# A hybrid decoder layer on one core: key and query weights loaded a pair ahead, samples' steps within the attention's filling, a copy moved to DVE

## The chip, the cores and the metric

The kernel runs on one core of a Trainium2 chip. A core has five engines that work side by side, each through its own instructions in order: PE (TensorE, the matmuls), ACT (ScalarE), DVE (VectorE), POOL (GpSimd) and SP (SyncE, which here only issues transfers). ACT and POOL issue transfers too, from the same queue of instructions in which their computing stands. All transfers are carried out by 16 DMA engines. The metric is the time of one execution in microseconds (us), the median of several runs.

## The reference

One layer is computed for two groups at once: a prompt of 512 tokens and eight samples of one token each, with shared weights. From a normed input `h`, three branches run in parallel (RG-LRU, a gated delta rule, latent attention), are merged by gates, and a feed-forward part follows. The parts that the change touches are the causal convolution of four taps and the prompt's latent attention:

```python
def causal_conv(u, buf, w):
    T = u.shape[1]
    up = jnp.concatenate([buf.astype(u.dtype), u], axis=1)
    y = up[:, 0:T] * w[0]
    for j in range(1, CONV_W):
        y = y + up[:, j:j + T] * w[j]
    return y, up[:, T:]

def mla_prompt_attention(q_nope, q_rope, c_kv, k_rope, w_ukv):
    kv = jnp.einsum('bsc,cf->bsf', c_kv, w_ukv).reshape(B, S, H, QK_NOPE + V_HEAD)
    k_nope, v = kv[..., :QK_NOPE], kv[..., QK_NOPE:]
    ...
    s = (q_nope @ k_nope + q_rope @ k_rope) * MLA_SCALE      # 8 heads, causal
    p = softmax(s)
    return p @ v
```

The samples attend to 4096 cached positions each, in 128-row pages of `cache_ckv` and `cache_krope` that a page table names: scores against the pages, softmax, and a weighted sum of the pages, 32 pages a sample.

## The kernel before

All large products are made in three matmuls: each float32 weight tile is loaded into `raw` (two slots, `load`, L151), split by ACT into a high part `whi` (L158) and by DVE into the rest `wlo` (L159), two slots each; the activations are split in the same way (`hilo`, L179 and L180). PE then adds hi x hi, hi x lo and lo x hi in PSUM (`gemm`, L172).

Tokens lie along the free dimension, features on the 128 partitions. The stages in order of time: modulation and norm; the gated delta rule with its 24 convolutions (`prepare`), up to about 480 us; the RG-LRU branch with ten more convolutions (`lru_steps`) together with the samples' delta rule; the latents' products and the prompt's attention, about 737 to 925 us; three merges (`merge`), the output product, and the feed-forward part to the end.

The convolution (`conv`) puts 35 columns of state in front of the 512 columns of the prompt in a tile `cin` (two slots): POOL copies the state (L383), ACT the prompt (L384), DVE the samples' new column (L386); ACT and DVE then compute the four taps (L387 to L393).

The samples' attention is cut into 42 steps by a generator. `steps(n)` adds n to a count and runs as many steps as it then holds. The numbers of steps a call are `STEPS = (0.8, 0.7, 0.8, 0.7, 0.4, 1.2)`: index 5 for each pair of heads, 1 for each of the 16 rounds of the attention, 2 for the merges. A step of scores (L1112, tile `sp`) uses one block of pages in `cc`, which holds two blocks; the loads of the next block, eight of 144 KB, are issued as one becomes free: POOL issues numbers 1, 3 and 5 (`POOLED`, L1080), SP the other five (L1085). Every second step multiplies the weights with value pages (L1144, tile `sa`), which POOL loads into four tiles `cv` of 512 KB (L1127).

The latents' stage (from L1316 on) loads the stored latents `d_ck` and `d_cq` into `bf` (two slots, L1325, on SP) and splits them; `values` makes the values of all heads with `w_uv` (L1301, copied by ACT at L1303); then for each of four pairs of heads comes a key product and two query products (`lat_gemm`, L1312, two PSUM tiles `mm`), with `w_uk` (256 columns) and `w_uq` (768 columns) loaded by ACT's queue through `raw`. The key product is copied by ACT into `kt` (L1339), the query products are multiplied by DVE into `qt` (L1346).

The attention runs 18 rounds, i from -2 to 15: `attend` of round i, `turn` (transposes, L1377) of round i + 1 and `scores` (L1359, softmax at L1362 to L1367) of round i + 2. The rounds -2 and -1 fill this pipeline and end with `continue`, ahead of `steps(STEPS[1])`.

The order of each engine's instructions is not that of the text alone. A planner at build time goes by the program's order as priority, but takes what is ready by its own estimate of durations, and gives out the slots of the tiles; on the chip the order of each engine is then fixed. An instruction that waits holds all behind it on its engine. Pools that are opened later lie where closed ones lay, and their tiles wait for the last user of the place.

Of the kernel before, what the change touches and what calls it, by code (L numbers as in the profile page):

```python
# [9 lines left out]
F32 = mybir.dt.float32  # L10
# [13 lines left out]
NT = 2 * HB  # L24
# [78 lines left out]
def emit(es, tc, I, O):  # L103
# [43 lines left out]
    queue = [SP]  # L147
# [14 lines left out]
    def wload(src, n):  # L162
        return split(load(src, n), n)
# [153 lines left out]
    with ExitStack() as pha:  # L317
# [61 lines left out]
        def conv(p, pt, state, w, bias, nb, y):  # L379

            cin = p.tile([128, 548], F32, tag="cin", name="cin", bufs=2)
            y2 = p.tile([128, CW], F32, tag="cw", name="cz", bufs=6)
            G.tensor_copy(cin[:, 0:35], state)  # L383
            A.activation(view2(cin[:, 35:547]), pt[:, :, 0:256], AF.Copy)  # L384
# [902 lines left out]
    with ExitStack() as sub:  # L1287
# [5 lines left out]
        def values(lat):  # L1293
            uvs = [wload(I["w_uv"][c], 1024) for c in range(2)]
            for b in range(4):
                pt = mm_tile()
                for c in range(2):
                    xh, xl = lat["ck", c]
                    for i, (x, w) in enumerate(((xh, uvs[c][0]), (xh, uvs[c][1]), (xl, uvs[c][0]))):
                        for a in range(2):  # L1300
                            TE.matmul(pt[:, a, :], x[:, off(b):off(b) + 128], w[:, a * 512:(a + 1) * 512],  # L1301
                                      start=c == 0 and i == 0, stop=c == 1 and i == 2)
                A.activation(view2(vv[:, b]), pt, AF.Copy)  # L1303
                steps(STEPS[4])
# [11 lines left out]
        with ExitStack() as sub2:  # L1316
# [3 lines left out]
            krp = pl.tile([128, 512], F32, name="krp")  # L1320
            lat = {}
            for nm, src, n in (("ck", d_ck, 2), ("cq", d_cq, 3)):
                for i in range(n):
                    f = pl.tile([128, NT], F32, tag="bf", name="bf", bufs=2)
                    SP.dma_start(f, src[i])  # L1325
                    lat[nm, i] = hilo(pl, f, f"{nm}{i}", bufs=1)
# [7 lines left out]
            for p in range(4):  # L1334
                pt = lat_gemm(lat, wload(I["w_uk"][p], 256), 0, "ck", 2)
                kt = ph.tile([128, 2, 512], F32, name=f"kt{p}")
# [4 lines left out]
                kts.append(kt)  # L1341
                wq = wload(I["w_uq"][p], 768)
                for u in range(2):
# [49 lines left out]
        for i in range(-2, 16):  # L1393
# [7 lines left out]
            if i + 2 < 16:  # L1401
                Ps[i + 2] = scores(*order[i + 2])
            if i < 0:
                continue
            steps(STEPS[1])
            if 8 <= i < 13:
# [415 lines left out]
```

## Time and profile before

| | before |
|---|---|
| median of 3 runs | 1553.57 us (1547.87 to 1562.55) |
| profiled execution, its time | 1555.39 us |
| its span, first to last instruction | 1553.6 us |
| instructions | 33507 |
| moved by DMA | 255.98 MB, mean 165 GB/s |

The page gives the busy time of each engine over the span; the other views give the same execution by wait, by stretch of time, or instruction by instruction. The granted clock is that of PE, as a share of full speed. `ACTq` and `SPq` are the instruction queues of ACT and SP where transfers are issued.

### The profile page before, as it was taken

The page shows a single profiled execution, that of the slowest core. Times are in us where ns is not written, and L with a number is a line of the kernel's source. Part 1 is how long each engine was busy: PE and PEld are TensorE (multiplying, and loading weights), DVE is VectorE, ACT ScalarE, POOL GpSimd, SP SyncE. Part 2 cuts the span into 40 slices and gives each one's busy share as a digit, 9 for nine tenths or more (in the row PEclk, how much of TensorE's full clock was granted, in tenths as well). Part 3 has the DMA queues.
Part 4 walks back from the last instruction along what each step waited for, and adds up shares of the span by engine and source line. Part 5 has one row for each costly group of instructions (what it writes and reads, how often), then busy time and mean ns, then how long its engine had stood idle before and what let it go on. Part 6 is the DMA issues. An engine that isn't in the chain of part 4 may idle for free.

```text
span 1553.6 us, 33507 instructions
## 1 busy us (share of the span) xinstructions
PE 1479.3 (95%) x13348; PEld 1346.7 (87%) x13348; DVE 818.9 (53%) x1938; ACT 643.1 (41%) x1226; POOL 243.2 (16%) x391
## 2 busy tenths in 40 slices
PE   8999999999998999999878889999999999999997
PEld 5799999999987988887665559999999999999997
DVE  4577865857755676765344424464464333333333
ACT  4464644644533777564334433232243222222233
POOL 0121000100103444333323532000000000000001
PEclk7999999999998999999889999999999999999998
DMA  8234142351436966877777978676743223323222
GB/s 344 83 112 122 58 127 95 97 155 61 125 117 196 270 194 210 275 235 249 241 234 198 265 248 292 192 240 216 270 151 109 84 86 86 103 93 95 84 84 93
DMA packets 117774, 255.98 MB, mean 165 GB/s; under 512 B 22281, under 2 KB 53770, under 8 KB 117618
## 3 DMA queue, kind: packets, MB, share of 16 engines
q1 hardware_dynamic: 83904, 161.85, 33.0%
q0 software_dynamic: 13824, 47.72, 9.9%
q10 hardware_dynamic: 19890, 44.27, 8.8%
q8 instruction: 105, 1.72, 0.5%
q14 instruction: 51, 0.42, 0.1%
HBM read 228.61 MB, written 25.18 MB: 163 GB/s over the span
## 4 chain that ended last, share of the span: by engine, by line
PE 51%; DMA 4%; issue 2%; ACT 2%; DVE 1%; another core or an unknown queue 1%; SPq 0%; POOL 0%; ACTq 0%; POOLq 0%; DVEq 0%
PE mm L172 40%; PE sp L1112 2%; PE sa L1144 1%; DMA bf<-d_ro 1%; PE s L224 1%; PE ho L1387 1%; PE h L1359 1%; DMA St<-in_S 1%; PE mm L1312 1%; DMA bf<-d_cq 1%; PE h L1377 1%; DMA out_gS_s<-St 1%; PE s L888 1%; DMA raw<-in_w_rg 1%
## 5 line engine op out<-in xcount | busy, mean ns | idle before, releaser
L158 ACT ACTIVATE whi<-raw 128x1024 fp32r<-128x1024 f32 (+3 forms) x204 | 199.5, 979 | 506.9 <-PE mm L172 443.6
L159 DVE TENSOR_TENSOR wlo<-raw,whi 128x1024 fp32r<-128x1024 f32 (+3 forms) x204 | 229.1, 1124 | 232.4 <-ACT whi L158 226.4
L172 PE MATMUL mm<-hh,whi 128*128 128x260 f32 x1312 | 281.1, 292 | 4.9 <-ACT hh L295 2.7
L172 PE MATMUL mm<-hh,wlo 128*128 128x260 f32 x1312 | 273.5, 287 | 0.1
L172 PE MATMUL mm<-hl,whi 128*128 128x260 f32 x1312 | 272.9, 287 | 0.7 <-DVE hl L295 0.6
L172 PEld LDWEIGHTS mm<-hh,whi 128*128 128x128 f32 x1312 | 206.8, 191 | 16.6 <-issue 7.9
L172 PEld LDWEIGHTS mm<-hl,whi 128*128 128x128 f32 x1312 | 206.1, 191 | 3.2 <-issue 2.1
L172 PEld LDWEIGHTS mm<-hh,wlo 128*128 128x128 f32 x1312 | 206.1, 191 | 3.0 <-issue 1.4
L172 PE MATMUL mm<-h2h,whi 128*128 128x260 f32 x704 | 144.5, 284 | 0.0
L172 PE MATMUL mm<-h2h,wlo 128*128 128x260 f32 x704 | 144.1, 283 | 0.0
L172 PE MATMUL mm<-h2l,whi 128*128 128x260 f32 x704 | 143.6, 283 | 0.0
L1080 POOL DMA_INDIRECT cc<-in_ckvT,pkx x96 | 101.6, 1058 | 129.6 <-PE sp L1112 74.3
L172 PE MATMUL mm<-brh,whi 128*128 128x260 f32 x556 | 114.2, 287 | 5.1 <-ACT brh L179 4.9
L172 PE MATMUL mm<-brl,whi 128*128 128x260 f32 x556 | 113.0, 284 | 0.7 <-issue 0.6
L172 PE MATMUL mm<-brh,wlo 128*128 128x260 f32 x556 | 112.3, 284 | 0.0
L172 PEld LDWEIGHTS mm<-h2h,whi 128*128 128x128 f32 x704 | 109.3, 188 | 2.9 <-issue 2.5
L172 PEld LDWEIGHTS mm<-h2h,wlo 128*128 128x128 f32 x704 | 109.4, 188 | 0.4 <-issue 0.4
L172 PEld LDWEIGHTS mm<-h2l,whi 128*128 128x128 f32 x704 | 109.1, 188 | 0.4 <-DVE h2l L1549 0.4
L172 PEld LDWEIGHTS mm<-brh,whi 128*128 128x128 f32 x556 | 86.0, 189 | 11.0 <-ACT brh L179 6.0
L172 PEld LDWEIGHTS mm<-brl,whi 128*128 128x128 f32 x556 | 85.9, 189 | 1.6 <-DVE mx L1120 0.8
L172 PEld LDWEIGHTS mm<-brh,wlo 128*128 128x128 f32 x556 | 86.0, 189 | 0.3 <-issue 0.2
L1610 POOL TENSOR_TENSOR x<-x,rf 128x260 f32<-128x260 f32 x6 | 4.3, 736 | 514.7 <-ACT rf L1607 514.7
(522 smaller groups left out, 2500.7 us busy)
## 6 DMA issues: line engine op xcount, KB each, us to landing
raw<-in_w_in SPq DMA_DIRECT2D x55, 512.0 KB
wa<-in_w_ada SPq DMA_DIRECT2D x48, 512.0 KB
cc<-in_ckvT SPq DMA_DIRECT2D x160, 144.0 KB
raw<-in_w_f SPq DMA_DIRECT2D x44, 512.0 KB
raw<-in_w_in ACTq DMA_DIRECT2D x27, 512.0 KB
raw<-in_w_f SPq DMA_DIRECT2D x16, 384.0 KB
d_g<-gt ACTq DMA_DIRECT2D x22, 260.0 KB
raw<-in_w_rg ACTq DMA_DIRECT2D x16, 320.0 KB
```

The source lines that it names most:

```text
L158: A.activation(hi[:, :n], raw[:, :n], AF.Copy)
L159: V.tensor_tensor(lo[:, :n], raw[:, :n], hi[:, :n], ALU.subtract)
L172: TE.matmul(pt[:, a, 0:HB], w[:, k * 128:k * 128 + 128], x[k0 + k][:, a * HB:(a + 1) * HB], start=start and k == 0 and i == 0, stop=stop a ...
L224: TE.matmul(pt[32 * j:32 * j + 32, 0:256], sc[:, k, :], wa[:, j * 256:(j + 1) * 256], start=k == 0, stop=k == 7)
L888: TE.matmul(pw[:, 0:272], a_[:, sl], b_[:, ca], start=i == 0, stop=i == 2)
L1080: G.indirect_dma_start(ct[:, i].rearrange("p c t -> p (c t)"), None, I["ckvT"], bass.IndirectOffsetOnAxis(ap=pkx[0:96, o:o + 1], axis=0))
L1112: TE.matmul(po[32 * j:32 * j + 32, 0:256], Qst[:, t, 4 * self.g + j, :], cts[j][:, :, t, :], start=t == 0, stop=t == 2)
L1144: TE.matmul(self.pa[32 * j:32 * j + 32, 0:256], self.PTt[:, t * 128 + 32 * j:t * 128 + 32 * j + 32], self.vts[j][:, t * 256:(t + 1) * 256] ...
L1312: TE.matmul(pt[:, a, 0:256], a_[:, c0 + k * 128:c0 + k * 128 + 128], x[:, a * HB:a * HB + 256], start=k == 0 and i == 0, stop=k == n - 1 a ...
L1359: TE.matmul(pS[:, 0:n], qts[2 * p + u][:, b * 128:n], kts[p][:, u, 0:n], start=True, stop=False)
L1377: TE.transpose(pT[:, kb * 128:(kb + 1) * 128], Ps[u][:, kb * 128:(kb + 1) * 128], ident)
L1387: TE.matmul(po[u][:, b * 128:(b + 1) * 128], vv[:, kb, hd * 128:(hd + 1) * 128], PTs[u][:, kb * 128:(kb + 1) * 128], start=kb == 0, stop=k ...
```

## The change

Three edits. In `conv` the state is copied by DVE instead of POOL. In the latents' stage the weights of the pairs get tiles of their own in the pool `pl`: `ruk`, four slots of 256 columns, and `ruq`, two of 768; the loads for pairs 0 and 1 are issued before the latents' loads, those of pair p + 2 after the split of pair p's query weights; `w_uv` is loaded ahead of them, and `bf` has three slots. In the attention `steps(STEPS[1])` moves above the `continue`, so that it also runs in rounds -2 and -1.

```diff
-            G.tensor_copy(cin[:, 0:35], state)
+            V.tensor_copy(cin[:, 0:35], state)
...
-            uvs = [wload(I["w_uv"][c], 1024) for c in range(2)]
+            uvs = [split(r, 1024) for r in raws]
...
+            raws = [load(I["w_uv"][c], 1024) for c in range(2)]
+            ruk, ruq = [], []
+
+            def key_load(p):
+                ruk.append(pl.tile([128, 256], F32, tag="ruk", name="ruk", bufs=4))
+                queue[0].dma_start(ruk[-1], I["w_uk"][p])
+
+            def query_load(p):
+                ruq.append(pl.tile([128, 768], F32, tag="ruq", name="ruq", bufs=2))
+                queue[0].dma_start(ruq[-1], I["w_uq"][p])
+
+            for p in range(2):
+                key_load(p)
+                query_load(p)
             for nm, src, n in (("ck", d_ck, 2), ("cq", d_cq, 3)):
                 for i in range(n):
-                    f = pl.tile([128, NT], F32, tag="bf", name="bf", bufs=2)
+                    f = pl.tile([128, NT], F32, tag="bf", name="bf", bufs=3)
...
             for p in range(4):
-                pt = lat_gemm(lat, wload(I["w_uk"][p], 256), 0, "ck", 2)
+                pt = lat_gemm(lat, split(ruk[p], 256), 0, "ck", 2)
...
-                wq = wload(I["w_uq"][p], 768)
+                wq = split(ruq[p], 768)
+                if p < 2:
+                    key_load(p + 2)
+                    query_load(p + 2)
...
+            steps(STEPS[1])
             if i < 0:
                 continue
-            steps(STEPS[1])
```

## Rows read from the trace of the kernel before

**Rows 1.** The page, part 1: busy us of each engine (share of the span), instructions.

```profile
PE 1479.3 (95%) x13348; PEld 1346.7 (87%) x13348; DVE 818.9 (53%) x1938; ACT 643.1 (41%) x1226; POOL 243.2 (16%) x391
```

**Rows 2.** Waits of PE, 762 to 816: us in total, times, longest.

```profile
PE mm L1312 <- ACT kt L1339: 6.1, 1, 6.1
PE h L1359 <- DVE qt L1346: 2.2, 1, 2.2
```

**Rows 3.** Stretches: length, busy us of each engine (instructions), clock, DMA share, GB/s.

```profile
737.00:749.00 12.00, 6.72 (x49) 3.39 (x45) 2.03 (x4) 3.92 (x8) 8.71 (x9) 0.71 1.00 323
...
758.00:767.00 9.00, 7.58 (x47) 5.04 (x45) 3.62 (x6) 6.38 (x10) 0.92 (x1) 1.00 0.29 83
763.00:806.10 43.10, 35.55 (x345) 29.61 (x346) 14.34 (x33) 13.95 (x27) 14.22 (x15) 0.92 0.75 233
806.10:815.00 8.90, 6.27 (x44) 3.71 (x46) 6.23 (x21) 4.16 (x11) 1.87 (x2) 0.81 0.53 162
...
838.00:912.00 74.00, 66.27 (x612) 42.47 (x613) 33.78 (x111) 30.41 (x88) 37.46 (x40) 1.00 0.87 259
```

**Rows 4.** Timeline of ACT: start, us, instruction [idle before <- releaser].

```profile
767.97 0.34 ACTq L151 DMA_DIRECT2D raw<-in_w_uk  x1
...
774.40 0.33 ACTq L151 DMA_DIRECT2D raw<-in_w_uq  x1
...
782.92 0.42 ACT L158 ACTIVATE whi<-raw 128x256 fp32r<-128x256 f32 x1 [4.94 <-remote]
783.24 0.57 ACT L1339 ACTIVATE kt<-mm 64x512 f32<-64x512 f32 x1
```

**Rows 5.** Timeline of PE around the stall: start, us, instruction, idle before.

```profile
768.76 0.40 PE L1312 MATMUL mm<-cq0h,whi 128*128 128x256 f32 x2
...
770.64 0.40 PE L1312 MATMUL mm<-cq2h,wlo 128*128 128x256 f32 x2
...
784.47 0.80 PE L1312 MATMUL mm<-cq0h,whi 128*128 128x256 f32 x2 [6.12 <-ACT kt L1339]
...
788.05 0.63 PE L1312 MATMUL mm<-cq2h,wlo 128*128 128x256 f32 x2
...
790.53 1.90 PE L1144 MATMUL sa<-cv,PT 128*32 128x256 f32 x32
```

**Rows 6.** Timeline of POOL: first of four issues of value pages.

```profile
772.77 0.95 POOL L1127 DMA_INDIRECT cv<-in_ckv,vix  x1 [3.29 <-PE sa L1144]
```

**Rows 7.** Timelines of ACT and of DVE at the attention's filling.

```profile
796.59 0.33 ACTq L151 DMA_DIRECT2D raw<-in_w_rg  x1
...
806.09 1.56 ACT L158 ACTIVATE whi<-raw 128x640 fp32r<-128x640 f32 x2 [2.85 <-DMA raw<-in_w_rg]
...
810.43 0.37 ACT L1365 ACTIVATE Pt<-h,mxp 128x128 f32<-128x128 f32 x1 [2.78 <-DMA raw<-in_w_rg]
...
806.86 0.82 DVE L159 TENSOR_TENSOR wlo<-raw,whi 128x640 fp32r<-128x640 f32 x1 [1.59 <-ACT whi L158]
...
808.00 0.68 DVE L1346 TENSOR_TENSOR qt<-mm,csq 128x512 f32<-128x512 f32 x1
```

**Rows 8.** Timelines of ACT and of SP at the start of the stage.

```profile
738.73 0.33 ACTq L151 DMA_DIRECT2D raw<-in_w_uq  x1
739.11 0.38 ACT L1115 ACTIVATE SC<-sp 128x256 f32<-128x256 f32 x1 [3.80 <-issue]
...
739.68 0.84 SPq L1325 DMA_DIRECT2D bf<-d_ck  x2
```

**Rows 9.** By line: state copies (ns min/median/max), who waited; pages, 480 to 736.

```profile
L383 POOL COPY cin<-gst x24: 211/213/1050, 66.4 to 394.2; 128x35 f32<-128x35 f32 x24
...
L386 DVE COPY cin<-mm x34: 152/165/174, 73.5 to 668.2; 128x8 f32<-128x8 f32 x34
...
POOL cin L383: 3.7, 1
...
L1080 POOL DMA_INDIRECT cc<-in_ckvT,pkx x52 | 59.9, 1153 | 68.5 <-PE sp L1112 28.9 <-ACT cin L384 12.3 <-issue 8.0
```

## The prediction

> **What bounds the kernel now.** I read the page's busy shares first, then what TensorE (PE) waited for, then the stretches of the part that the change touches, then the timelines of ACT, PE, DVE, SP and POOL inside them. PE is busy for 1479.3 of 1553.6 us [rows 1], so the whole kernel has 74 us to give, and only work that fills or removes a PE gap, or that keeps its clock up, can change the time. Of the waits of PE the longest single one is 6.1 us for `kt`, and another of 2.2 us for `qt` [rows 2]; both lie between 737 and 815 us, where the prompt's latents become keys and queries. The stretches show the same [rows 3]: 737 to 749, the start of the stage, has PE busy for 6.72 of 12.00 us at a granted clock of 0.71, with the DMA engines full (1.00, 323 GB/s); 758 to 767 has the DMA engines nearly idle (0.29); 763 to 806.1, the four pairs of heads, has PE idle for 43.10 - 35.55 = 7.55 us; 806.1 to 815, the filling of the attention, idles for 2.63 us. From 838 to 912, the attention itself, 7.7 us of 74 are idle.
>
> **The change part by part.** The sum is made against the profiled execution's own time, 1555.39 us (span 1553.6 and 1.8 around it). That is 1.8 us above the median of the runs, 1553.57, and I take those 1.8 us off at the end.
>
> *Loads of the pairs' weights.* In `before`, `w_uk` and `w_uq` go through the two slots of `raw`, so the load of pair 2's `w_uk` can be issued only at 767.97, after pair 1's split has given its slot back. Its split starts at 782.92, with ACT idle for 4.94 us before it [rows 4]. ACT works in order, and the copies of pair 1's `kt` out of PSUM stand behind that split, at 783.24; with two `mm` tiles, PE's next product has no PSUM until then. That is the 6.1 us of [rows 2]. The price has a second part. The nine pairs of matmuls of one query product take from 768.76 to 770.64 + 0.40 = 2.3 us undisturbed, and from 784.47 to 788.05 + 0.63 = 4.2 us after the stall [rows 5]: each takes 0.63 instead of 0.40 us, the level of 1.2 instead of 2.4 GHz after PE has stood still for 6 us. So the stall costs 6.1 + 1.9 = 8.0 us. After the change pair 2's key weights have a slot of their own from the start (four slots of `ruk`), and no load of pair 1 goes in front of them; the query weights of pair 2 are issued behind the split of pair 0, so before 767.97 instead of at 774.40 [rows 4]. The transfers between 758 and 767 find DMA engines at 0.29 [rows 3]. I take the whole stall as gone: **-8.0**; the bounds are 0 (the load lands as late as before) and -8.0.
>
> What is late next? With PE 8 us earlier, the samples' value product behind this stage would start at 790.53 - 8.0 = 782.5 (790.53 is its start, [rows 5]). Its four value tiles of 512 KB are issued by POOL from 772.77 on, one every 1.25 us [rows 6], to 777.7; 2.1 MB at the stretch's 233 GB/s [rows 3] is 9.0 us, so they land between 782 and 787. They may hold PE for 0 to 4.5 us; I take **+1.5**. Pair 3's loads are issued behind pair 1's split, near 774; at the 782.92 - 767.97 = 15 us that pair 2's `w_uk` took [rows 4] they land at 789. Without the stall a pair takes (43.1 - 8.0) / 4 = 8.8 us and the last begins at 806.1 - 8.0 - 8.8 = 789.3 [rows 3]: just in time.
>
> *The slots of `raw` set free.* Because the pairs no longer use `raw`, the first two loads of `w_rg` can be issued as soon as the values' weights are split, about 736, instead of 796.59. Before, ACT waits 2.85 us for the first of them at 806.09; behind ACT's split DVE's `wlo` of 806.86 stands in front of the last `qt`, 808.00, and this `qt` is PE's wait of 2.2 us. A second wait, 2.78 us, holds the first softmax at 810.43 [rows 7, 2]. *The samples' steps within the filling*: the line moves above the `continue`, so 2 x 0.7 = 1.4 steps more run in the filling, and every later one comes 1.4 steps sooner. They bring their transfers with them: one block of pages is eight loads of 144 KB, five on SP, three on POOL. It is the same PE work in another place. It saves only what gap it fills. Both edits draw on one gap: PE idles 2.63 us in 806.1 to 815, and its clock of 0.81 costs 6.27 x 0.19 = 1.2 us more [rows 3]. I take **-2.5** for both together; bounds 0 and -3.8. Later in the attention the extra lead can fill gaps or meet pages that have not landed; with the engines at 0.87 there [rows 3] I take 0 for that.
>
> *The start of the stage.* Here the signs oppose. A third slot of `bf` starts the first query latent's load with the key latents', and the new tiles lie ahead of `bf` in the pool, so its place changes. The first of these loads was issued at 739.68 [rows 8]; what `bf` waits for in its new place may end sooner. The upper bound of the gain is the whole idle time and clock loss of 737 to 749: 5.28 + 6.72 x 0.29 = 7.2 us [rows 3]. Against it, pair 1's weights (128 + 384 KB) and two pieces of `w_rg` (640 KB) move into a stretch with full DMA engines: 1.18 MB at 323 GB/s is 3.7 us [rows 3]. Also four loads instead of two stand on ACT's queue there. Already one, issued at 738.73, has softmax work of the samples behind it (`SC`, 739.11, idle 3.80 [rows 8]); a load that waits for its place holds all of ACT. I take **0**, with the bounds -7.2 and +3.7.
>
> *The convolution's state by DVE.* 34 copies of 128x35 leave POOL (0.21 us each, the longest 1.05) and go to DVE, where the nearest row is the copy of 128x8 in the same convolution, 0.165 us: 34 x 0.165 = 5.6 us [rows 9]. DVE is busy for 53% [rows 1], and a copy can run as soon as the buffer's last reader on DVE is done. The one wait for POOL's copy that the trace shows is 3.7 us of DVE [rows 9], at the first convolution of the recurrent branch, where PE was waiting for pages. I take **0**; bounds -3.7 and +5.6. The row also shows that POOL's copy can grow fivefold; it does not show beside what.
>
> That agrees with the Trainium skill, "SBUF — State Buffer", section "Who interferes with whom": an fp32 copy from SBUF to SBUF on DVE and a GpSimd instruction exclude each other for the length of the one that began first. By that rule the move makes DVE wait for POOL where POOL used to wait for nobody, most of all in the recurrent branch, with POOL issuing pages. The sum by the rows is 0 here; by the rule it would be what the rival below works out.
>
> **Sum**: -8.0 + 1.5 - 2.5 = -9.0, so 1546.4 against 1555.39, and 1544.6 on the scale of the median: I say 1545.
>
> **The rivals.**
>
> *The start of the stage gains too.* If the latents come as early as their new place and slot allow, up to 7.2 us go in addition: 1545 - 7 = 1538. For it speaks that PE has only 6.72 us of work in 12 us there; against it, that the DMA engines are full.
>
> *Nothing gained, the transfers only change places.* Pages and weights share the engines, and these are at 0.75 to 1.00 in most stretches [rows 3]. If the pages' values take the place of the stall in full (4.5), and the extra 1.18 MB cost 3.7 in the full stretch, the sum is -8.0 + 4.5 - 2.5 + 3.7 = -2.3: 1551.3. Against it: the 43.1 us x 233 GB/s = 10.0 MB of 763 to 806.1 would be 31 us at 323 GB/s, so the engines have room for a stage 8 us shorter.
>
> *Slower: `w_rg` takes a slot of `whi`.* Its raw data now lie ready 60 us before they are used, and `whi` has two slots. If the planner splits a piece as soon as a slot is free, one slot is held until the merge, and each pair's two splits can no longer run under a product: ACT and DVE for 256 columns 0.4 + 0.4, for 768 columns 0.8 + 1.0 [the row of 128x256 is in rows 4, scaled by columns with the piece of 640 in rows 7] = 2.6 us a pair, 10.5 us for four: 1545 + 10.5 = 1555.5, 2 us slower. It decides from the second pair on whether the gain survives: taken ahead of the first pair it eats all of it, taken after the last it costs nothing. Against it: the pairs' splits come earlier in the program and are then ready too.
>
> *DVE's copies wait for POOL.* In the recurrent branch 10 copies can each meet a page issue of 1.153 us [rows 9]: 11.5 us of DVE. If all of it reached PE: 1556.5. Against it: PE hardly waits for DVE in that stretch; no wait of the kind is among the longest of [rows 2]. The rule of the Trainium skill cited above is what speaks for this one.
>
> **How the numbers follow.** Forecast 0.52, start gains too 0.24, nothing gained 0.14, `whi` 0.06, DVE behind POOL 0.04. The likeliest case's own range is 1539 to 1551. To hold 8 in 10 it is widened to the lower half of the second case and to the slower rivals: 1533 to 1558; the planner orders everything anew, which moves small waits by a few us either way and is within this. One per cent is 15.5 us, about what a measurement of this kernel can tell from no change. Faster by more than that (below 1538) needs the second case's better half and a good tail of the first: 0.2. Slower by more than that (above 1569) needs two rivals at once: 0.04. The rest, 0.76, is within 1%.
>
> **What would show it.** The wait of PE for `kt` of 6 us gone, and pair 2's query product with 0.40 us a pair of matmuls throughout; `whi` of pair 2 without idle ACT before it; `w_rg` issued before 760, and no ACT wait for it ahead of the first softmax; `bf` from `d_ck` issued before 740 (second case) or after (first). Wrong: a new PE wait of more than 4 us for `cv` between 780 and 790; ACT idle for more than 4 us behind a load of `ruk` or `ruq`; splits of pairs 1 to 3 that start only when a product has ended.

## The result, and the profile after

The changed kernel takes 1569.47 us (median of 17 runs, 1564.89 to 1577.23), the kernel before 1555.87 in the same session (17 runs): a ratio of 1.0108, 95% interval 1.0090 to 1.0126. It is slower by 1.1%, 24 us above the 1545 that I predicted and above the upper end of 1558. The profiled execution has a span of 1568.8 us against 1553.6.

Both kernels cut at the same five events. Windows of before, then of after: from the first transposition of the latents' stage to the first value product, to the first key product, to pair 1's key product, to the first score of the attention, to its last product. Columns: length, busy us of PE (instructions), PEld, DVE, ACT, POOL, clock, DMA share, GB/s.

```profile
737.06:748.90 11.84, 6.57 (x49) 3.29 (x45) 2.03 (x4) 3.92 (x8) 8.64 (x9) 0.71 1.00 323
748.90:763.16 14.26, 13.20 (x50) 10.06 (x49) 5.50 (x12) 5.07 (x7) 0.07 (x1) 0.88 0.78 236
763.16:774.56 11.40, 11.03 (x118) 7.93 (x118) 4.46 (x7) 4.47 (x7) 4.25 (x5) 1.00 0.56 166
774.56:806.12 31.56, 24.54 (x233) 21.69 (x229) 9.86 (x26) 9.40 (x19) 9.98 (x11) 0.89 0.82 258
806.12:910.88 104.76, 88.85 (x779) 56.76 (x778) 50.37 (x161) 45.00 (x125) 45.36 (x48) 0.95 0.80 232
```

```profile
737.66:749.95 12.29, 4.04 (x33) 2.05 (x30) 0.74 (x3) 2.64 (x5) 8.38 (x9) 0.68 1.04 340
749.95:770.17 20.22, 15.68 (x48) 11.98 (x49) 7.10 (x14) 6.57 (x10) 0.00 (x0) 0.78 0.69 223
770.17:783.59 13.42, 13.10 (x134) 9.09 (x132) 4.06 (x6) 5.07 (x8) 3.59 (x4) 1.00 0.41 124
783.59:816.09 32.50, 24.68 (x230) 21.76 (x230) 10.55 (x28) 9.36 (x19) 10.58 (x12) 0.84 0.74 223
816.09:930.05 113.96, 98.81 (x810) 61.01 (x812) 49.00 (x162) 46.05 (x126) 48.58 (x52) 0.91 0.78 234
```

The stage starts at the same place (737.06, 737.66), so the 700 us ahead of it, where the convolution lies, cost nothing. Then the lengths differ by +0.45, +5.96, +2.02, +0.94 and +9.20; from the last product of the attention to the end of the span the changed kernel is 4.0 us shorter (1568.8 - 930.05 against 1553.6 - 910.88). The sum is 14.6 us, and the stage's start 0.6 later makes it the 15.2 between the spans. Two places carry it: the values with the first pair (+8.4 together with the stage's start), and the attention less what comes back behind it (+5.2).

The first place. Of the +5.96 in the values, 3.5 is PE standing still (20.22 - 15.68 against 14.26 - 13.20) and 2.5 is PE slower at a clock of 0.78 for 0.88. ACT's timeline, then PE's (start, us, instruction, idle before and what ended it):

```profile
749.26 0.64 ACT L179 ACTIVATE ck0h<-bf 128x520 fp32r<-128x520 f32 x1 [6.90 <-DMA ruk<-in_w_uk]
...
756.83 1.03 ACT L1303 ACTIVATE vv<-mm 128x1024 f32<-128x1024 f32 x1 [0.90 <-DMA ruk<-in_w_uk]
763.33 0.64 ACT L179 ACTIVATE cq1h<-bf 128x520 fp32r<-128x520 f32 x1 [5.48 <-DMA bf<-d_cq]
764.12 0.64 ACT L179 ACTIVATE cq2h<-bf 128x520 fp32r<-128x520 f32 x1 [0.16 <-DMA bf<-d_cq]
764.66 1.92 ACT L1303 ACTIVATE vv<-mm 128x1024 f32<-128x1024 f32 x2
```

```profile
760.55 0.63 PE L1301 MATMUL mm<-whi,ck1l 128*128 128x512 f32 x2
765.72 1.11 PE L1301 MATMUL mm<-whi,ck0h 128*128 128x512 f32 x2 [4.54 <-ACT vv L1303]
766.63 1.06 PE L1301 MATMUL mm<-wlo,ck0h 128*128 128x512 f32 x2
```

PE needs a PSUM tile and waits for the copy `vv`; the copy stands on ACT behind two splits, and the first of these waits for `bf<-d_cq` until 763.33. In the kernel before the same split started here:

```profile
757.98 0.64 ACT L179 ACTIVATE cq1h<-bf 128x520 fp32r<-128x520 f32 x1 [1.80 <-DMA bf<-d_cq]
```

After the standstill in the changed kernel a pair of matmuls takes 1.06 instead of 0.63 us, the lower of the two clock levels. The DMA queues in the first 20 us of the stage, before (737.06 to 757.06), then after (737.66 to 757.66): q1 is SP's, q10 ACT's, q0 POOL's; packets, MB, share of 16 engines.

```profile
q1 hardware_dynamic: 1655, 2.90, 47.5%
q0 software_dynamic: 865, 2.98, 44.0%
q10 hardware_dynamic: 260, 0.58, 10.1%
```

```profile
q0 software_dynamic: 876, 3.02, 44.7%
q1 hardware_dynamic: 1218, 2.22, 33.4%
q10 hardware_dynamic: 892, 1.70, 25.5%
```

ACT's queue moves 1.12 MB more, SP's, which carries the latents, 0.68 MB less.

And the stall that the change was to remove is there: `kt`, 7.0 us (before 6.1, [rows 2]). PE, then ACT, of after:

```profile
794.46 0.80 PE L1312 MATMUL mm<-cq0h,whi 128*128 128x256 f32 x2 [7.04 <-ACT kt L1354]
```

```profile
754.54 0.35 ACTq L1328 DMA_DIRECT2D ruk<-in_w_uk  x1
...
792.90 0.42 ACT L158 ACTIVATE whi<-ruk 128x256 fp32r<-128x256 f32 x1 [4.90 <-remote]
```

The third load of `ruk`, 754.54, is pair 2's. Its split starts after 4.90 us of idle ACT, as it did in [rows 4] after 4.94, though its weights were issued 38 us ahead of it.

### The profile page after: what moved, and what is told of

It reads as the page before. It is cut to its first block, busy times and chain, and to the rows that moved or that the text cites. A ratio compares the mean times of both kernels' runs of the same rounds, so it can differ in the third digit from the quotient of the medians.

```text
span 1568.8 us, 33462 instructions
## 1 busy us (share of the span) xinstructions
PE 1487.9 (95%) x13348; PEld 1349.5 (86%) x13348; DVE 821.9 (52%) x1972; ACT 644.4 (41%) x1226; POOL 226.5 (14%) x357
## 4 chain that ended last, share of the span: by engine, by line
PE 52%; DMA 4%; issue 2%; DVE 2%; ACT 2%; another core or an unknown queue 1%; POOL 0%; SPq 0%; POOLq 0%; ACTq 0%; DVEq 0%
PE mm L172 40%; PE sp L1112 2%; PE sa L1144 2%; PE ho L1405 1%; PE s L224 1%; PE mm L1312 1%; DMA cc<-in_ckvT 1%; PE h L1377 1%; DMA ruq<-in_w_uq 1%; PE s L888 1%; PE h L1395 1%; DMA bf<-d_ro 1%; DMA bf<-d_og 1%; DMA cv<-in_ckv,vix 0%
## 5 line engine op out<-in xcount | busy, mean ns | idle before, releaser
L158 ACT ACTIVATE whi<-raw 128x1024 fp32r<-128x1024 f32 (+2 forms) x196 | 194.5, 993 | 503.2 <-PE mm L172 464.2
L159 DVE TENSOR_TENSOR wlo<-raw,whi 128x1024 fp32r<-128x1024 f32 (+2 forms) x196 | 223.7, 1142 | 213.8 <-ACT whi L158 207.8
L172 PEld LDWEIGHTS mm<-hh,whi 128*128 128x128 f32 x1312 | 206.5, 190 | 15.9 <-issue 7.6
```

Source lines behind the costliest of these rows:

```text
L158: A.activation(hi[:, :n], raw[:, :n], AF.Copy)
L159: V.tensor_tensor(lo[:, :n], raw[:, :n], hi[:, :n], ALU.subtract)
L172: TE.matmul(pt[:, a, 0:HB], w[:, k * 128:k * 128 + 128], x[k0 + k][:, a * HB:(a + 1) * HB], start=start and k == 0 and i == 0, stop=stop a ...
```

## The experiments

The runs were made on five chips, called A to E. The table: ratio to the kernel before on the same chip; "keys", the us from the first transposition to pair 1's key product, by the profiled execution; MB on ACT's queue in the first 20 of them; the wait for `kt`; and "late signals", worked out from the PE, DVE and POOL rows: of the samples' blocks of scores whose last product starts while POOL issues a train of three or more indirect loads, or up to about 2 us after it, in how many DVE's `mx<-sp` starts over 1 us later than both the start of that product and the end of DVE's own work ahead of it.

| kernel | chip | ratio (95%) | keys | MB | `kt` | late signals |
|---|---|---|---|---|---|---|
| before | | | 37.5 | 0.58 | 6.1 | 5 of 14 |
| after | | 1.0108 (1.0090 to 1.0126) | 45.9 | 1.70 | 7.0 | 3 of 12 |
| e1_conv | A | 0.9994 (0.9966 to 1.0023) | 36.8 | 0.64 | 1.5 | 5 of 13 |
| e2_steps | A | 1.0025 (0.9990 to 1.0061) | 37.3 | 0.54 | 6.1 | 1 of 12 |
| e3_load | A | 1.0057 (1.0035 to 1.0078) | 47.0 | 1.79 | 7.3 | 4 of 14 |
| e4_load_bf2 | A | 1.0031 (1.0008 to 1.0055) | 47.1 | 1.76 | 7.2 | 4 of 14 |
| e6_hold | B | 1.0027 (1.0002 to 1.0052) | 42.7 | 1.36 | under 1 | 0 of 16 |
| e7_one | B | 1.0033 (1.0001 to 1.0066) | 39.1 | 1.10 | under 1 | 0 of 18 |
| e8_ruk2 | B | 1.0054 (1.0027 to 1.0081) | 41.2 | 1.32 | under 1 | 0 of 17 |
| e9_deep | B | 0.9985 (0.9958 to 1.0011) | 37.7 | 0.46 | under 1 | 0 of 18 |
| b_again | C | 0.9993 (0.9970 to 1.0016) | 36.9 | 0.56 | 5.9 | 5 of 15 |
| p0_pages_sp | C | two runs, 1.0126 (1.0038 to 1.0214) | 38.9 | 0.42 | 2.0 | 4 of 6 |
| a1_ruk2 | C | 1.0112 (1.0065 to 1.0160) | 46.2 | 1.77 | 7.1 | 3 of 11 |
| d1_deep_steps | C | 1.0034 (0.9998 to 1.0069) | 37.3 | 0.54 | under 1 | 2 of 13 |
| f1_after_one | D | 1.0096 (1.0064 to 1.0127) | 44.8 | 1.31 | 7.4 | 3 of 10 |
| f2_after_behind | D | 1.0128 (1.0100 to 1.0156) | 44.2 | 1.85 | 7.3 | 3 of 10 |
| f3_deep | D | 1.0003 (0.9976 to 1.0030) | 36.9 | 0.63 | under 1 | 5 of 14 |
| f4_pages8 | D | one run, 1585.41 us | 38.6 | 0.56 | under 1 | 3 of 16 |
| g1_after_order | E | 1.0115 (1.0086 to 1.0144) | 45.2 | 1.83 | 7.2 | 3 of 10 |
| g2_order_nosteps | E | 1.0073 (1.0050 to 1.0096) | 44.0 | 1.82 | 7.2 | 5 of 15 |

Counted from the modelled end of the last product, the late ones are fewer by one in nine of the kernels, and the second number shifts by one or two with where a train's edges are set. No block that ends elsewhere is late. The kernel before has a median of 1557.1 on A, 1539.4 on B, 1549.0 on C, 1553.0 on D and 1554.2 us on E.

**One part at a time** (A). Theory: the loads hold the loss; rivals: the copies, or the steps. e1:

```diff
-            G.tensor_copy(cin[:, 0:35], state)
+            V.tensor_copy(cin[:, 0:35], state)
```

> The kernel before with one edit: DVE instead of POOL copies the convolution's state. Theory (the loads and the steps cost, the copies are free): 1556 us, within 0.3% of before. Rival (the copies' order on DVE costs all through the recurrent stage): 1562 to 1572 us, with the loss spread over the stretch before 737 us; the trace of the changed kernel is against it, since its latents' stage starts only 0.6 us late.

e2:

```diff
+            steps(STEPS[1])
             if i < 0:
                 continue
-            steps(STEPS[1])
```

> The kernel before with one edit: the line of the samples' steps stands above the continue in the attention's loop. Theory (the lead fills the filling of the attention but meets pages that have not landed later): 1553 to 1559 us, the filling's idle time (2.6 us between 806 and 815) smaller and the attention longer by the 5 us that the changed kernel lost between its first and last product of values by probabilities beyond the moved work. Rival (that loss belongs to the early loads): 1552 to 1554 us, with the attention's length changed by the moved work (about 4 us) alone and the merges shorter by as much.

e3 is the rest of the diff; e4 is e3 with two slots of `bf`:

> The kernel before with the loads' part alone: weights of the prompt's keys, queries and values loaded ahead into tiles of their own, three slots of bf; copies by POOL and steps where they were. Theory: this part holds the whole loss, +10 us up to the first score as in the changed kernel (first key product 7 us late, the wait for kt in front of pair 2's queries still 6 to 7 us), so 1564 to 1570 us. Rival (the moved steps and copies bring the loss): 1551 to 1558 us.

```diff
-                    f = pl.tile([128, NT], F32, tag="bf", name="bf", bufs=3)
+                    f = pl.tile([128, NT], F32, tag="bf", name="bf", bufs=2)
```

> The same loads' part, but with two slots of bf as before. Theory A (the third slot starts the query latents' loads and their splits too early, in front of the copies of the values out of PSUM on ACT): the first key product comes 5 to 7 us sooner than with three slots, 1557 to 1561 us. Theory B (the early weights on ACT's queue and on the full DMA engines cost, whatever the slots of bf): as with three slots, 1564 to 1570 us. In both the wait for kt in front of pair 2's query product stays at 6 to 7 us, if its cause is not the late load of the weights.

The copies are free. The loads hold the larger part; with two slots of `bf` "keys" is 47 as with three, and the intervals of the two ratios overlap. The steps cost 0.25%, not to be told from nothing by this run alone. The three parts add up to 0.76% where the whole change costs 1.08%, which is within their intervals. By the profiles e2 lengthens the attention by 5.4 us, and little comes back: its merges have 3.1 us less of samples' scores and turns, but PE now meets value pages that have not landed. Waits of PE in e2, 910 to 1000 us (total, times, longest); before has no such wait there:

```profile
PE sa L1144 <- DMA cv<-in_ckv,vix: 2.4, 2, 2.2
```

The early loads alone also bring something. The attention from its first score to its last product, in e1 (which has neither the loads nor the steps), e3 and e4, with the columns of the windows above:

```profile
798.01:902.80 104.79, 88.69 (x780) 56.69 (x779) 50.42 (x161) 44.54 (x124) 45.13 (x48) 0.97 0.78 233
825.24:927.92 102.68, 92.77 (x781) 57.29 (x782) 49.35 (x160) 44.55 (x124) 45.41 (x48) 0.95 0.80 236
813.52:914.41 100.89, 88.96 (x779) 56.53 (x779) 49.17 (x160) 44.60 (x124) 45.04 (x48) 0.98 0.79 239
```

It is 2.1 and 3.9 us shorter, with less idle PE: about what I had expected of the freed slots, though which part of the loads' edit does it was not separated.

e1 has a second result. Its stall for `kt` is 1.5 instead of 6.1 us, with the code of this stage untouched and `w_uk` going through `raw` as before, issued 9.3 us ahead of its split. POOL's train there is of seven loads, as in the kernel before (768.86 to 777.63), and ACT's split comes in the middle of it. Behind the stall PE now waits for value pages. ACT's split, the last of POOL's train, and PE's waits (total, times, longest):

```profile
773.31 0.42 ACT L158 ACTIVATE whi<-raw 128x256 fp32r<-128x256 f32 x1 [1.61 <-PE mm L1312]
776.71 0.92 POOL L1080 DMA_INDIRECT cc<-in_ckvT,pkx  x1 [0.30 <-issue]
PE sa L1144 <- DMA cv<-in_ckv,vix: 2.4, 1, 2.4
PE mm L1312 <- ACT kt L1339: 1.5, 1, 1.5
```

**Which of the early loads** (B). e6 keeps the `raw` slots in use until pair 3, so `w_rg` is not early:

```diff
+                if p == 3:
+                    V.tensor_tensor(kept[:, 0:1], raws[0][:, 0:1], kts[2][:, 0, 0:1], ALU.mult)
...
+                if p == 3:
+                    V.tensor_tensor(kept[:, 1:2], raws[1][:, 0:1], kts[2][:, 1, 0:1], ALU.mult)
```

> The loads' part alone (three slots of bf), with one tiny DVE operation that keeps the two raw slots in use until pair 3, so that the first two loads of w_rg (640 KB) stay where they were before. Theory 1 (bytes moved into the full DMA engines at the start of the latents' stage delay bf<-d_cq): values stage (first value product to its end) shorter than with the loads' part alone (22.4 us) by 2 to 4 us, total 1560 to 1563 us. Theory 2 (ACT stands in its queue at the issues of ruk for pairs 2 and 3, each of which waits for an earlier transfer, and the copies vv stand behind it): values stage stays at 20 to 23 us, total 1564 to 1568 us.

e7 loads one pair ahead, with two slots of `ruk`; e8 only gives `ruk` two slots. Both start from e3:

```diff
-            for p in range(2):
+            for p in range(1):
...
-                if p < 2:
-                    key_load(p + 2)
-                    query_load(p + 2)
+                if p < 3:
+                    key_load(p + 1)
+                    query_load(p + 1)
```

> The loads' part alone, but a single pair ahead: pair 0's weights at the start, pair p+1's behind the split of pair p, two slots of ruk. This takes 512 KB of pair 1 and 256 KB of pairs 2 and 3 out of the start, though the planner still issues pair 1's key weights ahead of the first copy vv. Theory 1 (bytes): values stage 17 to 20 us, total 1559 to 1562 us. Theory 2 (ACT held at issues ahead of vv): values stage 17 to 20 us too, since three of the four early issues are gone or moved, the wait of ACT ahead of the first vv under 2 us. If neither holds, 22 us and 1566 us as with the loads' part alone.

```diff
-                ruk.append(pl.tile([128, 256], F32, tag="ruk", name="ruk", bufs=4))
+                ruk.append(pl.tile([128, 256], F32, tag="ruk", name="ruk", bufs=2))
```

> The loads' part alone with two slots of ruk instead of four: nothing changes at the start but that the key weights of pairs 2 and 3 (128 KB each) are issued behind pair 0's and pair 1's splits, not ahead of the first copy vv. Theory 1 (bytes): 256 KB less are worth under 1 us, values stage 20 to 22 us, total 1565 to 1567 us. Theory 2 (ACT held at issues): the wait of ACT ahead of the first vv (1.4 to 4.7 us behind ruk) goes, values stage 16 to 19 us, total 1560 to 1563 us.

e9 is the kernel before with five PSUM tiles of one bank in place of two of two banks, so that PE can run further ahead of ACT (the value products take two of them, with two copies; the halves of a key or query product follow each other instead of taking turns):

```diff
-            psum(sub2, "psl", mm=2, s=1)
+            psum(sub2, "psl", lm=5, s=1)
...
-            pt = mm_tile()
+            pt = s_tile("lm").rearrange("p (a b) -> p a b", a=2)
```

> The kernel before with one edit: the latents' stage uses five PSUM tiles of one bank (s=1 beside them) instead of two tiles of two banks; a key or query product fits in one bank, a value product takes two. Theory (the stall for kt is a round trip: PE's signal to ACT comes late while POOL issues its seven indirect loads of samples' pages, 772.77 to 781.36 in the kernel before, ACT's split starts 1.6 us after their end, and PE has only two tiles to work ahead in): PE runs on into pair 2's two query products, the wait for kt of 6.1 us falls under 2 us, pairs' stage 37 to 39 us instead of 43.5, total 1549 to 1553 us. Rival (PE lacks the split weights as well, so the wait only changes its name): a wait for whi or wlo of 4 to 6 us a product later, total 1555 to 1558 us.

The totals expected were those of a slower chip, so stretches and ratios are compared. On this chip "keys" is 39 to 43 us with early loads, 37.7 without. The smallest amount on ACT's queue (e7) loses least, 1.4 us. The values stage of e8 was 16.1 us, as its theory 2 said, that of e6 23.2. This seemed to settle on ACT standing at the issues of `ruk`, until a1 below. And no signal is late on this chip, and none of the four kernels waits over 1 us for `kt`, though e6 and e8 have that part as the changed kernel has it. So e9 could not test its theory here.

With the stall gone, the stage is still no shorter: in its place PE waits for the value pages of the product behind it. PE's waits in e6, e7, e8 and e9, 755 to 825:

```profile
PE sa L1144 <- DMA cv<-in_ckv,vix: 5.3, 4, 2.2
PE sa L1144 <- DMA cv<-in_ckv,vix: 6.4, 4, 3.4
PE sa L1144 <- DMA cv<-in_ckv,vix: 4.7, 3, 1.8
PE sa L1144 <- DMA cv<-in_ckv,vix: 4.3, 2, 2.5
```

From pair 1's key product to the first score e6, e7 and e8 take 30.8 to 32.0 us, about as long as the kernel before with its stall (31.6).

**The stall, on a chip that has it** (C). b_again is the kernel before; p0 issues no direct pages on POOL:

> The kernel before, unchanged, to have its trace beside the three others of this call. Theory (the stall for kt is not in the program but in how late a signal of PE arrives while POOL issues its indirect loads): DVE's mx<-sp starts more than 1 us after the last score product of its block in 3 to 5 of some 13 blocks that end while POOL issues, and the stall for kt is 4 to 7 us, or, as in the four kernels of the second call (no mx later than 1 us), both are absent. Rival (the stall hangs on the late load of w_uk): the stall of 6 us is there whether mx is late or not.

```diff
-POOLED = (1, 3, 5)
+POOLED = ()
```

> The kernel before with all eight direct loads of a block of pages on SP: POOL's train of indirect loads in the pairs' stage is four instead of seven. Theory (PE's signals are held until 1.0 to 1.6 us after the last of POOL's train): where the other kernel of this call shows late signals, the stall for kt shrinks from 6.1 to 1 to 3 us, since the train ends 3.7 us earlier. Rival (late load, or full DMA engines whoever issues): the stall stays at 5 to 7 us. The total is open: SP has 60 percent more loads to issue, 1550 to 1580 us.

POOL and ACT of b_again (the last of seven indirect loads; the split), then POOL, DVE and PE of p0 (the last of four):

```profile
777.99 0.92 POOL L1080 DMA_INDIRECT cc<-in_ckvT,pkx  x1 [0.30 <-issue]
...
780.39 0.42 ACT L158 ACTIVATE whi<-raw 128x256 fp32r<-128x256 f32 x1 [3.48 <-remote]
```

```profile
772.48 0.94 POOL L1127 DMA_INDIRECT cv<-in_ckv,vix  x1 [0.30 <-PE mm L1312]
...
774.47 0.42 DVE L1114 TENSOR_REDUCE mx<-sp 128x1 f32<-128x256 f32 x1 [5.94 <-remote]
...
776.75 0.50 PE L1312 MATMUL mm<-cq0h,whi 128*128 128x256 f32 x2 [1.95 <-ACT kt L1339]
```

In b_again POOL's train ends at 778.91 and ACT goes on 1.48 us later. In the changed kernel POOL's last issue (790.38, 0.92) ends at 791.30 and ACT goes on at 792.90, 1.60 later; in before 781.36 and 782.92 [rows 4], 1.56. In 13 of the 16 traces with late signals ACT's split at this place comes 1.5 to 1.8 us after the train's last issue; in e1 and f3 it comes within the train, and in p0 behind a late `mx`. With a train of four, p0 has its release 1.05 us after the end (773.42, 774.47), and the stall is 1.95 us, as expected; but e1 has 1.5 with a train of seven, so one profile of each length does not show that the length sets the stall. (p0 as a whole is slower: SP now carries all pages.)

Nor are all signals held to the train's end. In the changed kernel's own train DVE goes on 4.1 us ahead of it:

```profile
787.17 0.42 DVE L1114 TENSOR_REDUCE mx<-sp 128x1 f32<-128x256 f32 x1 [7.25 <-remote]
790.38 0.92 POOL L1080 DMA_INDIRECT cc<-in_ckvT,pkx  x1 [0.30 <-issue]
```

Of the 58 late signals in the table 30 come while POOL still issues, 2.6 to 5.2 us ahead of its last, and the others 0.6 to 1.8 us after it.

The trace also records when the semaphore is counted up by which PE tells that a product is done. In the changed kernel the matmuls that end pair 1's key product are over at 785.28 (a modelled end) and their two updates are recorded at 792.88 and 792.92; in e9, on B, each lies within 0.02 us of the product's end. So it is the signal that is late, not ACT that is slow to see it. The traces differ in one thing more: those of B hold practically all updates (e9: 1130 records for 1128 instructions of PE that make one, 13150 by DMA), those of the other chips lack some (before: 1096 for 1123, 10482 by DMA). Whether the recording itself delays the signals was not tested.

f4 (D) has a train of eight:

```diff
-POOLED = (1, 3, 5)
+POOLED = (1, 3, 5, 7)
```

> The kernel before with four of the eight direct loads of a block of pages on POOL instead of three: its train in the pairs' stage is eight indirect loads. Theory (signals of PE are held until the train is over): where signals are late, the stall for kt is 6.5 to 8 us (6 with seven, 2 with four) and its release comes 1.4 to 1.6 us after the train's end. Rival: 6 us as with seven, or a release that does not follow the train's end. The total is open.

```profile
804.13 1.29 DVE L1346 TENSOR_TENSOR qt<-mm,csq 128x512 f32<-128x512 f32 x2 [7.44 <-remote]
```

The train ends at 802.54 (its last issue: 801.62, 0.92), the release follows 1.59 us later, as expected. But the stall for `kt` did not grow, it was gone: the copies of `kt` (796.20) came through ahead of the standstill, DVE's `qt` waited 7.44 us in their place, and PE had samples' work to do. So a release soon after the train's last issue came again, but not the stall forecast for a longer train; whom the delay hits depends on where the others stand.

**Back to the loss of the changed kernel** (C and D). a1 is the changed kernel with e8's edit, f1 with e7's; f2 puts the loop of the first two pairs' loads behind the loads of the latents:

> The changed kernel with two slots of ruk instead of four, so that the key weights of pairs 2 and 3 are issued behind the splits of pairs 0 and 1 and not ahead of the first copy vv. Theory (ACT stands at these two issues, which wait for earlier transfers, with the copies vv behind it): values stage 16 to 18 us instead of 20.4, total 3 to 5 us under the changed kernel, a ratio of 1.007 to 1.009 to the kernel before. Rival (the two issues only fill a wait that bf<-d_cq would make anyway): ratio 1.010 to 1.011.

> The changed kernel, but one pair of weights ahead instead of two (two slots of ruk): pair 1's 512 KB are issued only behind the splits of the key latents. Theory A (pair 1's weights stand between the latents' loads on full DMA engines; bf<-d_cq lands later, ACT's splits cq1h and cq2h wait for it and the copies vv stand behind them): from the first transposition to the end of the values 26 to 28 us instead of 32.7, ratio to before 1.004 to 1.007, the rest being the moved steps. Theory B (early w_rg, or the order of cq1h and cq2h ahead of the second vv, whatever the bytes): 31 to 33 us, ratio 1.009 to 1.011.

```diff
-            for p in range(2):
-                key_load(p)
-                query_load(p)
             for nm, src, n in (("ck", d_ck, 2), ("cq", d_cq, 3)):
...
             SP.dma_start(krp, d_kr)
+            for p in range(2):
+                key_load(p)
+                query_load(p)
```

> The changed kernel with the loop that issues the first two pairs' weights moved behind the loop over the latents' tiles; the planner still issues pair 0's ahead of the splits of the key latents and pair 1's query weights behind the first of them. Theory A: 28 to 31 us from the transposition to the end of the values, since half of pair 1 is still early, ratio 1.006 to 1.009. Theory B (order of ACT): cq1h stands ahead of the first vv here, so 32 to 34 us, ratio 1.010 to 1.013.

None gives the time back. a1 refutes the theory of the two issues: its ACT goes straight from `SC` to the first `vv`, and then stands 8.13 us at `cq1h`:

```profile
761.28 0.64 ACT L179 ACTIVATE cq1h<-bf 128x520 fp32r<-128x520 f32 x1 [8.13 <-DMA bf<-d_cq]
```

f1 did not really test pair 1's bytes: the planner issued them at 756.49 and 759.48, still ahead of the landing of `d_cq` (765.77).

**The order of ACT** (E). g1 lays down that each split of `cq` stands behind a copy `vv`; g2 also takes the moved steps back (e2's edit reversed):

```diff
-            values(lat)
+            values(lat, copies)
+            for i, f in late:
+                with tc.issue_after(copies[i].ins):
+                    lat["cq", i] = hilo(pl, f, f"cq{i}", bufs=1)
```

> The changed kernel with an order of ACT laid down: split cq0h behind the first copy vv, cq1h behind the second, cq2h behind the third; the loads stay. Theory B (PE waits for vv, which stands behind cq1h and cq2h, which wait for bf<-d_cq): the wait of PE for vv of 4.5 to 6.8 us goes, from the first transposition to the end of the values 26 to 28 us instead of 31.9 to 33, a part of it coming back at the first query product if cq2h is late; ratio to before 1.003 to 1.006. Rival (the transfers themselves are late, whatever waits for them: the value products also run at half clock and wait for ck1h): 30 to 33 us, or the same loss a product later at the first query product; ratio 1.008 to 1.011.

> The same order of ACT, with the line of the samples' steps back behind the continue: what stays of the change is the early loads with three slots of bf and the copies by DVE. If the order and the steps are the two shares of the loss: ratio 0.999 to 1.002. If the transfers are what is late: 1.004 to 1.007, as with the loads' part alone (1.0057).

ACT, then PE of g1:

```profile
764.97 0.64 ACT L179 ACTIVATE cq1h<-bf 128x520 fp32r<-128x520 f32 x1 [6.78 <-DMA bf<-d_cq]
```

```profile
767.40 0.79 PE L1312 MATMUL mm<-ck0h,whi 128*128 128x256 f32 x2 [4.70 <-ACT whi L158]
767.99 0.63 PE L1312 MATMUL mm<-ck0l,whi 128*128 128x256 f32 x2
```

The rival's numbers came. The value products run through (12.98 us from start to end instead of 20.4), but the latents land no sooner, and the same wait stands one product later, at the first key's split behind `cq1h`, with the lower clock until 776. "keys" is 45.2, hardly less than without the edit. The key product needs no `cq`; an order with its split ahead of `cq1h` was not run. From g1 to g2 the ratio falls by 0.0042: a second, larger reading of what the moved steps cost. The attention of g1, then of g2, at the same clock:

```profile
817.54:924.21 106.67, 91.26 (x810) 57.57 (x812) 48.56 (x162) 45.65 (x126) 48.72 (x52) 1.00 0.83 250
814.57:913.44 98.87, 88.02 (x779) 55.43 (x779) 49.22 (x160) 44.53 (x124) 45.00 (x48) 1.00 0.82 242
```

The moved steps make it 7.8 us longer, 3.2 of them more work and 4.6 more idle PE.

**Deeper PSUM** (C, D). d1 is e9 with e2's edit, f3 is e9 again:

> The kernel before with five single-bank PSUM tiles in the latents' stage and the line of the samples' steps above the continue. Theory (the first takes away the round trip through two tiles, the second fills the wait of the first transposition, 4.6 to 6.3 us, in the filling): ratio 0.993 to 0.998. Rival (the steps give back later in the attention what they fill, as the steps' move alone did, ratio 1.0025): 0.999 to 1.002.

> The same kernel as e9_deep (the kernel before with five single-bank PSUM tiles in the latents' stage), on another chip. Theory: on a chip that shows PE's late signals the wait for kt of 6 us falls under 2 us, pairs' stage 39 to 41 us instead of 42.3 to 43.5, ratio 0.996 to 0.998; on a chip without them 0.998 to 1.000 as before. Rival (the wait saved comes back at the first softmax of the attention, which waits for the last query tiles): 0.999 to 1.001 on either.

The stall is gone on both chips, with late signals in 5 of 14 blocks in f3; pair 1's key product to the first score is 29.2 us in f3 and 30.7 in b_again. The total does not move measurably: f3 has a wait of 2.6 us for value pages in the same stretch that b_again has not, and d1's ratio is 1.0034 with the steps moved as well; 0.996 to 0.998 and 0.993 to 0.998 had been expected. None of these versions is measurably faster than the kernel before.

## Why the prediction was wrong, step by step

**The stall of 8.0 us** is the step that failed. I read [rows 4] so that pair 2's split waited for its load, because the load was issued late and because no other cause was named; the row itself said only "remote". In the changed kernel the weights were issued 38 us ahead of the split and the stall was there; in e1 they were issued as late as ever and the stall was 1.5 us. What the runs show in its place: while POOL issues a train of indirect loads, signals of PE reach ACT and DVE late, in the traces of A, C, D and E `mx` by up to 5.5 us, and 1.8 us after the last issue at the latest they are there. That the train causes it is not shown: ACT's release 1.5 to 1.8 us after its last issue in 13 traces speaks for it, e1's 1.5 us with a train of seven and the 30 signals that come within a train against so simple a rule, and the missing records are a rival left open. The bound of 0 that I gave this step was the value: the stretch that holds it is 0.9 us longer.

The term behind it, +1.5 for value pages late next, is void in the changed kernel, where PE has no wait for `cv` between 780 and 790. But it was sized too small for the case that I forecast: wherever the stall is small or gone with the steps unmoved, in e1, f3, e6, e7, e8 and e9, PE waits 2.4 to 6.4 us for these pages (only p0 and f4, with other issuers of pages, have none). On B this is the sign of being wrong that I had set, a wait of over 4 us for `cv`. So part of the 8.0 would have gone to the pages without the late signals too.

**The start of the stage**, taken as 0 with a bound of +3.7, cost 8.4 us up to pair 1's key product. The bytes were sized rightly (1.18 MB; 1.12 more on ACT's queue in the first 20 us), and their price in transfer time not far off: `cq1h` could start 25.7 us after the transposition (763.33 - 737.66) for 20.9 before (757.98 - 737.06), 4.8 later. Missing was what a late transfer does behind it: ACT in order, the copies `vv` behind the splits, two PSUM tiles, so in the values PE stood still for 3.5 us more and lost 2.5 to the clock. (The first pair's 2 us are samples' work that the first stretch had done before; there PE is busy for 4.04 instead of 6.57 us, and the stretch is no shorter.) That every variant with over 1.3 MB on ACT's queue loses 3.4 to 10.3 us of "keys" against a kernel on its chip without early loads (E had none), and none with under 0.7 more than 2, fits, and g1 shows that the order of the copies `vv` alone is not it. How the loss grows with the bytes stays open: no run kept the own tiles and took all the early loads out, and chip B loses less than the others at the same 1.3 MB. The marker that I set for "wrong" came: ACT idle 6.90 us behind a load of `ruk`.

**The freed slots and the moved steps**, taken as -2.5. The wait for `qt` fell from 2.2 [rows 2] to 0.7 us and that for `w_rg` at the first softmax went; this much was right, and the loads alone shorten the attention by 2.1 and 3.9 us (e3, e4). The moved steps turned it round: the attention of the changed kernel is 9.2 us longer, of which 4.0 come back, and the steps cost 0.25% alone (e2, within its uncertainty of none) and 0.42% between g1 and g2. I had called them the same work in another place that fills gaps. They filled next to none: idle PE in the attention is 15.2 us for 15.9, while PE is busy for 10.0 us more, with 27 more matmuls of samples' scores and a clock of 0.91 for 0.95. What I set at 0, "meet pages that have not landed", came behind the attention, with 2.3 us for `cv`, as in e2 with 2.4; within it no wait for pages is listed.

**The copies by DVE**, taken as 0: right, 0.9994 with an interval of 0.3% either way. The Trainium skill, "SBUF — State Buffer", "Who interferes with whom", has DVE's copy and a GpSimd instruction exclude each other; no price of it shows in e1: one such copy takes 0.93 us where the median is 0.18, and no wait for any is listed.

**The rivals.** None is what happened. The slower one by `whi` was looked for in the wrong place: `w_rg` took a slot only at 811.79, behind the pairs. "Transfers only change places" came nearest, with pages in the place of the stall and a price at the start, and still kept the -8.0. Every case of the range had the stall gone, but that alone does not explain the miss: a case with the stall kept and the +3.7 would have stood near 1557, inside the range. The rest is what the start cost beyond its bound (8.4 for 3.7) and the attention's 5.2.

## What to carry to other kernels

A wait whose end the profile calls "remote" has no named cause: a load that is late beside it is a suspect, and moving that load is a test to make before it is a gain to count. Before counting a stall as gain, ask what PE would wait for next; here it was the value pages. Where DMA engines are full, an early load is paid by what it passes, and the price here was not its transfer time but that time plus the in-order engine behind the late transfer plus PE's lower clock afterwards. Work moved ahead into a gap brings its pages ahead too; look at where they are due next.

## What the runs showed of the hardware that was not expected

While POOL issues indirect loads in a row, DVE started on PE's results over 1 us late in 1 to 5 of 6 to 16 blocks on four chips and in none of 69 on the fifth (B); one and the same program has 5 of 14 on D (f3) and 0 of 18 on B (e9). The kernel before is 18 us faster on that chip than on A. The profiled wait for `kt` of one and the same code in the kernel before and in e1 is 6.1 and 1.5 us, so a single profile tells such a stall no better than that.
